# Every second wide block product of the FFNs multiplies the weights' low part first

## The chip, the cores and the metric

The kernel runs on one core of a Trainium2 chip. The metric is the device time of one execution in microseconds, the median of the runs of one measurement. Before the change it is 969.28 us (three runs, 968.81 to 969.39). The profile is of one further execution.

## The reference: what is computed

The input is a sequence of 512 tokens of 1024 channels in float32. Two decoder layers run over it. Each has a mixer (a gated convolution and pooling in the first, a gated MLP in the second) and then a gated FFN with 2816 hidden channels, and both add to the running state `h`. The change touches the FFNs alone:

```python
def gated_conv_ffn(x, w_gate, w_up, conv_w, conv_b, w_down):
    g = jnp.einsum('bsd,df->bsf', x, w_gate)
    g = causal_dwconv3(g, conv_w) + conv_b
    up = jnp.einsum('bsd,df->bsf', x, w_up)
    return jnp.einsum('bsf,fd->bsd', jax.nn.silu(g) * up, w_down)
```

So there are two products of 512 tokens by 1024 channels by 2816 hidden channels (gate, called `g` in the kernel, and up, called `u`), a convolution over three tokens, a silu, an elementwise product and a product back to 1024 channels (down).

## The kernel before: tiles, stages and order

**Two parts per number.** Matmuls take operands of the type float32r. Each operand is held as a high part (`hi`) and a rest (`lo`), and a product is the sum of three: hi by hi, hi by lo and lo by hi. The fourth, lo by lo, is left out.

**Block products.** The gate and up products are made with seven multiplications of half-size blocks instead of eight (a Strassen scheme). One block of work is a pair of hidden tiles, named by its first tile `f` = 2, 4, ..., 20 (`Ffn.products`, L885). In it each of `g` and `u` has seven products, so there are 14, in the order written in the loop at L920 to L922: g1, u1, g2, g5, g6, u5, u6, g7, u2, u7, g3, u3, g4, u4. The contraction of one product runs over four tiles of 128 channels (`NP` = 4, index `kp`). Weights stand in TensorE (they are what LDWEIGHTS loads, 128 by 128); activations stream through, and the result has 128 hidden channels by 256 tokens.

**Wide and narrow matmuls.** A product in the narrow form (L675 to L681) has twelve matmuls of 256 columns, all into one half of a PSUM bank. The wide form (L667 to L674, when `both` is given) uses that the hi and lo part of an activation lie side by side: four matmuls of 512 columns multiply the weights' hi part by both at once, and put hi by hi in the left half of the bank and hi by lo in the right half (L669). Then four matmuls of 256 columns multiply the weights' lo part by the activations' hi part into the left half (L672). Below, a wide matmul is one of 512 columns and a narrow one is one of 256. The halves are added afterwards by VectorE or by a copy on ScalarE and an add on VectorE (L905 and L917).

**Which products are wide.** `in_both` (L898) decides by `f`. In the first FFN all 14 products are wide for `f` = 8 to 20, in the second for `f` = 6 to 20, which makes 15 blocks. In one more block of each FFN (`f` = 6 and `f` = 4) the seven of `g` and u2, u5 and u3 are wide and the other four of `u` are narrow.

**Banks.** A product goes to bank `a`, `b` or `e` of its key (`BANK`, L652): 1, 6, 7 and 4 share `a`, 5 and 3 share `e`, and 2 has `b`. Later products add onto what is there; the first into a bank starts it anew.

**Where the low parts come from.** `Ffn.prepare` (L832) splits the weights of the next block while the current one is multiplied. ScalarE makes the hi parts. The lo parts are made by VectorE (`halves`, L828: the tiles `wlo_a`, `wlo_s12u`, `wlo_s34u`) or by a negated copy on ScalarE and an adding DMA from the POOL queue (L144 to L146 and L860 to L862: `wlo_g`, `wlo_u`, and for `g` also `wlo_s12g` and `wlo_s34g`).

**Order.** A tile scheduler sorts the instructions of each engine from its own estimate of when operands are ready; only what is put in `inorder` keeps the written order. So matmuls of neighbouring products can change places. After each block of work come matmuls of the down product (`half_down`, `mm3` at L159 to L161), all of 512 columns: 48 in a row after most blocks.

Of the kernel before, what the change touches and what calls it, by code (L numbers as in the profile page):

```python
# [31 lines left out]
def tile_trunk(ctx: ExitStack, tc: tile.TileContext, x, norm_mix, norm_ffn, final_norm,  # L32
# [3 lines left out]
    nc = tc.nc  # L36
# [9 lines left out]
    def mm_bank(name):  # L46
        return ps_mm.tile([P, 512], F32, tag="mm", name=name)
# [242 lines left out]
    def padded_tile():  # L290
        turn[0] += 1
        return padded[turn[0] % NPADDED]
# [296 lines left out]
    def project_blocks(name, w, acts, sums, norm, spare):  # L589
# [37 lines left out]
        for product in (1, 2, 5, 6, 3, 7, 4):  # L627
            for i in range(2):
                hi, lo = stat[product]
                c = slice(i * P, (i + 1) * P)  # L630
                if product == 3:
                    banks[i].pop("e")
                ps = multiply(banks[i], f"{name}_{product}{i}", product,
                              lambda kp: (hi[:, kp, c], lo[:, kp, c]),
                              lambda kp: moving(product, kp))
                for row, half in onto[product]:
                    d = h[4 + i + row][:, half * HALF : (half + 1) * HALF]
                    nc.vector.tensor_tensor(d, ps, d, ALU.add)
                if product in (3, 4):
                    norm.add(4 + i + 2 * (product == 4))  # L640
# [5 lines left out]
    NP = NK // 2  # L646
# [6 lines left out]

    last_matmul = [None]

    def multiply(banks, name, product, left, right, both=None):

        at = BANK[product]
        first = at not in banks
        if first:
            banks[at] = mm_bank(f"{name}{at}")
        ps = banks[at][:, :HALF]
        if both is not None:  # L667
            for kp in range(NP):
                nc.tensor.matmul(banks[at], left(kp)[0], both(kp), start=first and kp == 0,  # L669
                                 stop=kp == NP - 1, skip_group_check=True)  # L670
            for kp in range(NP):
                last_matmul[0] = nc.tensor.matmul(ps, left(kp)[1], right(kp)[0], start=False,  # L672
                                                  stop=kp == NP - 1, skip_group_check=True)
            return banks[at]  # L674
        for kp in range(NP):  # L675
            (a_hi, a_lo), (b_hi, b_lo) = left(kp), right(kp)
            for l, r, end in ((a_hi, b_hi, False), (a_hi, b_lo, False),
                              (a_lo, b_hi, kp == NP - 1)):
                nc.tensor.matmul(ps, l, r, start=first, stop=end, skip_group_check=True)  # L679
                first = False  # L680
        return ps  # L681
# [8 lines left out]
    class Ffn:  # L690
# [124 lines left out]
                return self.t41both[kp][:, :, product - 4, :]  # L815
            return hg2[kp + NP * (product > 1)][:, :, HALF * (product == 3) :][:, :, :HALF]

        def multiply(self, banks, name, product, weights_, both):
            hi, lo = weights_
            return multiply(banks, name, product, lambda kp: (hi[:, kp, :], lo[:, kp, :]),  # L820
                            lambda kp: self.moving(product, kp),
                            (lambda kp: self.moving_both(product, kp)) if both else None)

        def unit(self, name):
            return [wp.tile([P, 2, 4, P], F32R, tag=f"w{x}", bufs=6, name=f"w{x}_{name}")
# [59 lines left out]
        def products(self, f, stat):  # L885

            layer, ap, n = self.layer, self.ap, f"{self.layer}_{f}"
            banks = {"g": {}, "u": {}}
            kept = ap.tile([P, 3, HALF], F32, tag="kept", bufs=1, name=f"kept{n}")
            pads = [padded_tile() for _ in range(2)]  # L890
            lo, hi = slice(2, 2 + HALF), slice(2 + HALF, 2 + S)
            dst = {("g", 1): pads[0][:, lo], ("g", 6): pads[0][:, hi], ("g", 7): pads[1][:, hi],
                   ("g", 4): pads[1][:, lo]}
            dst.update({("u", product): kept[:, i, :] for i, product in enumerate((1, 6, 7))})
            onto = {2: 1, 7: 7, 3: 6}
            s = {}

            def in_both(key, product):  # L898
                first = FIRST_WIDE[layer]
                return f >= first[key] or f == first["g"] and product in (2, 5, 3)  # L900

            def add(d, bank, halves):
                ins = None
                for half in halves:
                    ins = nc.vector.tensor_tensor(d, bank[:, half * HALF : (half + 1) * HALF], d,  # L905
                                                  ALU.add)
                return ins

            def after(key, product, bank):
                halves = range(1 + in_both(key, product))  # L910
                if product in onto:
                    ins = add(dst[key, onto[product]], bank, halves)
                    if product == 7:
                        self.added[key] = ins
                elif (key, product) != ("u", 4):
                    d = dst[key, 7 if product == 5 else product]
                    nc.scalar.copy(d, bank[:, :HALF])  # L917
                    add(d, bank, halves[1:])

            for key, product in (("g", 1), ("u", 1), ("g", 2), ("g", 5), ("g", 6), ("u", 5),  # L920
                                 ("u", 6), ("g", 7), ("u", 2), ("u", 7), ("g", 3), ("u", 3),
                                 ("g", 4), ("u", 4)):  # L922
                bank = self.multiply(banks[key], f"{key}{n}", product, stat[key, product],
                                     in_both(key, product))
                after(key, product, bank)
                if (key, product) in (("g", 4), ("g", 3)):
                    j = product == 4
                    row = pads[j][:, 2:]
                    nc.vector.tensor_tensor(row, row, self.r, ALU.mult)  # L929
                    s[j] = self.silu(self.conv(pads[j], f + j), f + j)  # L930
                    if j and layer == 0:
                        nc.vector.tensor_tensor(s[1], s[1], self.r, ALU.mult)
            if layer == 0:
                nc.vector.tensor_tensor(kept[:, :2, :], kept[:, :2, :],
                                        self.r.rearrange("p (a b) -> p a b", a=2), ALU.mult)
            s0 = s[0].rearrange("p (a b) -> p a b", a=2)
            nc.vector.tensor_tensor(s0, kept[:, :2, :], s0, ALU.mult)
            nc.vector.tensor_tensor(s[1][:, HALF:], kept[:, 2, :], s[1][:, HALF:], ALU.mult)
            last = bank[:, :HALF]
            if in_both("u", 4):  # L940
                last = kept[:, 0, :]
                nc.scalar.copy(last, bank[:, :HALF])
                add(last, bank, (1,))
            nc.vector.tensor_tensor(s[1][:, :HALF], last, s[1][:, :HALF], ALU.mult)
            return [(f + 1, s[1]), (f, s[0])]
# [632 lines left out]
```

## Time and profile before

| what | value |
|---|---|
| median of three runs | 969.28 us |
| the profiled execution | 968.74 us |
| its span, first to last instruction | 967.0 us |
| TensorE matmul (PE) busy | 957.9 us, 5152 matmuls |
| weight loads (PEld) busy | 826.4 us |
| VectorE (DVE) / ScalarE (ACT) / GpSimd (POOL) busy | 847.5 / 622.7 / 161.6 us |
| granted TensorE clock, mean | 0.998 |

The profiled execution has 1.74 us around its span. A matmul's busy time overlaps that of the next one (a matmul of 512 columns is shown as 390 ns, though the next starts 227 ns after it in the longest stretches), so what a matmul takes from the stream is read from one start to the next start, in the timeline. A timeline row gives start, duration, engine, line, operation, output and inputs, shape and how many equal instructions it merges.

### The profile page before, as it was taken

The numbers are of one execution on the slowest core, as the hardware profiler recorded it, in microseconds if no ns is written. First come the engines' busy times: TensorE is split into PE (matmuls) and PEld (weight loads), VectorE is DVE, ScalarE is ACT, GpSimd is POOL, SyncE is SP. The second block draws the span as 40 slices with busy tenths as digits, with TensorE's granted clock in tenths as the row PEclk, the third lists the DMA queues.
The fourth block names the chain that finished last, engine by engine and source line by source line (L and its number), as shares of the span: only waits on it lengthen the run. The fifth ranks groups of instructions, "written<-read, shape, count | busy, mean of one in ns | idle before, by whom it ended". The sixth has DMA issues, their size and how long they took to land.

```text
span 967.0 us, 14196 instructions
## 1 busy us (share of the span) xinstructions
PE 957.9 (99%) x5152; PEld 826.4 (85%) x5152; DVE 847.5 (88%) x1435; ACT 622.7 (64%) x940; POOL 161.6 (17%) x183
## 2 busy tenths in 40 slices
PE   9999999999999999999999999999999999999996
PEld 7888898998888888888888888989888888888885
DVE  6887988989899898998878689899998989889898
ACT  5524667766576565765586847787665666656775
POOL 2141333111011010110311002311111011100123
PEclk9999999999999999999999999999999999999999
DMA  7442355787677677774352323567767777668775
GB/s 253 149 137 87 66 147 119 180 191 187 160 177 179 149 176 191 170 176 136 130 152 87 109 88 87 144 143 175 188 148 190 190 175 174 160 162 202 182 166 141
DMA packets 95825, 150.45 MB, mean 156 GB/s; under 512 B 5284, under 2 KB 61580, under 8 KB 95756
## 3 DMA queue, kind: packets, MB, share of 16 engines
q1 hardware_dynamic: 78284, 98.69, 32.5%
q0 software_dynamic: 15696, 49.03, 28.3%
q10 hardware_dynamic: 1776, 1.84, 0.6%
q8 instruction: 40, 0.66, 0.3%
q14 instruction: 29, 0.24, 0.1%
HBM read 98.42 MB, written 2.10 MB: 104 GB/s over the span
## 4 chain that ended last, share of the span: by engine, by line
PE 99%; DVE 1%; issue 0%; ACT 0%; POOLq 0%; DVEq 0%; POOL 0%
PE dn L160 3%; PE d L160 3%; PE dn L161 3%; PE d L159 3%; PE dn L159 3%; PE d L161 3%; PE vu_a L1127 2%; PE gu L159 2%; PE gu L161 2%; PE gu L160 2%; PE u_2a L679 1%; PE u_4a L679 1%; PE g_2a L679 1%; PE vu_e L1127 1%; PE dn_a L1426 1%; PE g_6a L669 1%
## 5 line engine op out<-in xcount | busy, mean ns | idle before, releaser
L146 POOL DMA_DIRECT2D wlo_g<-raw_g x20 | 17.2, 859 | 324.4 <-DVE kept L905 188.6
L715 DVE SCALAR_TENSOR_TENSOR c<-rows,prm,c 128x512 f32<-128x512 f32 x88 | 65.8, 749 | 1.1 <-ACT c L713 1.0
L160 PE MATMUL dn<-wlo_dn,a_hi 128*128 128x512 f32 x144 | 56.2, 391 | 0.0
L160 PE MATMUL d<-a_lo,whi_d 128*128 128x512 f32 x144 | 56.2, 390 | 0.0
L161 PE MATMUL dn<-whi_dn,a_lo 128*128 128x512 f32 x144 | 56.2, 390 | 0.0
L161 PE MATMUL d<-a_hi,wlo_d 128*128 128x512 f32 x144 | 56.2, 390 | 0.0
L159 PE MATMUL d<-a_hi,whi_d 128*128 128x512 f32 x144 | 56.2, 390 | 0.0
L159 PE MATMUL dn<-whi_dn,a_hi 128*128 128x512 f32 x144 | 56.1, 390 | 0.0
L829 ACT ACTIVATE whi_a<-raw_g 128x512 fp32r<-128x512 f32 x20 | 12.6, 632 | 61.3 <-PE g_8e L669 8.5
L144 ACT ACTIVATE wlo_g<-raw_g 128x1024 fp32r<-128x1024 f32 x20 | 21.2, 1062 | 26.4 <-PE g_2e L679 7.6
L1332 DVE SCALAR_TENSOR_TENSOR y<-dn,small,y 128x512 f32<-128x512 f32 x40 | 28.0, 749 | 8.6 <-PE dn L161 8.6
L713 ACT ACTIVATE c<-rows,prm 128x512 f32<-128x512 f32 x44 | 31.4, 715 | 5.3 <-DVE rows L929 5.3
L723 ACT ACTIVATE s<-c,prm 128x512 f32<-128x512 f32 x44 | 31.4, 716 | 3.4 <-DVE c L715 3.4
L268 ACT ACTIVATE a_hi<-s 128x512 fp32r<-128x512 f32 x40 | 24.8, 627 | 12.1 <-PE d L161 10.0
L204 ACT ACTIVATE hg<-h,prm 128x512 fp32r<-128x512 f32 x24 | 17.2, 718 | 23.5 <-DVE h L317 16.9
L155 DVE TENSOR_TENSOR wlo_dn<-raw_dn,whi_dn 128x1024 fp32r<-128x1024 f32 x18 | 22.0, 1224 | 11.7 <-ACT whi_dn L154 11.7
L161 PEld LDWEIGHTS dn<-whi_dn,a_lo 128*128 128x128 f32 x144 | 27.0, 188 | 5.7
L161 PEld LDWEIGHTS d<-a_hi,wlo_d 128*128 128x128 f32 x144 | 27.0, 188 | 5.7
L159 PEld LDWEIGHTS dn<-whi_dn,a_hi 128*128 128x128 f32 x144 | 27.1, 188 | 5.4
L159 PEld LDWEIGHTS d<-a_hi,whi_d 128*128 128x128 f32 x144 | 27.1, 188 | 5.3
L160 PEld LDWEIGHTS dn<-wlo_dn,a_hi 128*128 128x128 f32 x144 | 27.0, 188 | 5.4
L160 PEld LDWEIGHTS d<-a_lo,whi_d 128*128 128x128 f32 x144 | 27.1, 188 | 5.3
(1271 smaller groups left out, 3380.9 us busy)
## 6 DMA issues: line engine op xcount, KB each, us to landing
raw_g<-in_w_ffn_gate_dram SPq DMA_DIRECT2D x40, 512.0 KB, 3.8
raw_u<-in_w_ffn_up_dram SPq DMA_DIRECT2D x40, 512.0 KB, 4.7
raw_dn<-in_w_ffn_down_dram SPq DMA_DIRECT2D x22, 512.0 KB, 6.0
wlo_g<-raw_g POOLq DMA_DIRECT2D x20, 512.0 KB, 4.5
wlo_u<-raw_u POOLq DMA_DIRECT2D x20, 512.0 KB, 6.0
raw_d<-in_w_ffn_down_dram SPq DMA_DIRECT2D x18, 512.0 KB, 4.2
wlo_s12g<-s12g POOLq DMA_DIRECT2D x18, 512.0 KB, 6.3
wlo_s34g<-s34g POOLq DMA_DIRECT2D x18, 512.0 KB, 5.4
```

The lines of the kernel that those rows point to most:

```text
L144: first = nc.scalar.activation(lo, raw, AF.Copy, scale=-1.0)
L155: behind(nc.vector.tensor_tensor(lo, raw, hi.bitcast(F32), ALU.subtract), after[0])
L159: nc.tensor.matmul(ps, lhs[0], rhs[0], start=start, stop=False)
L160: nc.tensor.matmul(ps, lhs[0], rhs[1], start=False, stop=False)
L161: nc.tensor.matmul(ps, lhs[1], rhs[0], start=False, stop=stop)
L268: nc.scalar.activation(hi, src, AF.Copy, scale=scale)
L679: nc.tensor.matmul(ps, l, r, start=first, stop=end, skip_group_check=True)
L713: nc.scalar.activation(c, t[:, 0:S], AF.Copy, scale=prm("cf", ft))
L715: self.last_conv = nc.vector.scalar_tensor_tensor(c, t[:, i : S + i], prm("cf", i * NF + ft), c, op0=ALU.mult, op1=ALU.add)
L723: self.last_silu = nc.scalar.activation(s, c, AF.Silu, bias=self.prm("bf", ft))
L1127: nc.tensor.matmul(banks[at], lhs[l], rhs[r], start=first, stop=end, skip_group_check=True)
L1332: return nc.vector.scalar_tensor_tensor(dst, ps, ffn.cols[:, t : t + 1], dst, op0=ALU.mult, op1=ALU.add)
```

## The change

In every product with an odd index in the list of 14 (u1, g5, u5, g7, u7, u3, u4) the wide form is turned round: the four narrow matmuls of the lo part go first, then the four wide ones of the hi part. Products with an even index keep wide first. The first matmul of the product, whichever it is, starts a new bank. Products in the narrow form ignore the new argument. The number of matmuls, their operands, sizes and banks stay.

```diff
-    def multiply(banks, name, product, left, right, both=None):
+    def multiply(banks, name, product, left, right, both=None, low_first=False):
...
         if both is not None:
-            for kp in range(NP):
-                nc.tensor.matmul(banks[at], left(kp)[0], both(kp), start=first and kp == 0,
-                                 stop=kp == NP - 1, skip_group_check=True)
-            for kp in range(NP):
-                last_matmul[0] = nc.tensor.matmul(ps, left(kp)[1], right(kp)[0], start=False,
-                                                  stop=kp == NP - 1, skip_group_check=True)
+            for low in (low_first, not low_first):
+                for kp in range(NP):
+                    last_matmul[0] = nc.tensor.matmul(
+                        ps if low else banks[at], left(kp)[low],
+                        right(kp)[0] if low else both(kp), start=first, stop=kp == NP - 1,
+                        skip_group_check=True)
+                    first = False
             return banks[at]
...
-            for key, product in (("g", 1), ("u", 1), ("g", 2), ("g", 5), ("g", 6), ("u", 5),
-                                 ("u", 6), ("g", 7), ("u", 2), ("u", 7), ("g", 3), ("u", 3),
-                                 ("g", 4), ("u", 4)):
+            for i, (key, product) in enumerate((
+                    ("g", 1), ("u", 1), ("g", 2), ("g", 5), ("g", 6), ("u", 5), ("u", 6),
+                    ("g", 7), ("u", 2), ("u", 7), ("g", 3), ("u", 3), ("g", 4), ("u", 4))):
                 bank = self.multiply(banks[key], f"{key}{n}", product, stat[key, product],
-                                     in_both(key, product))
+                                     in_both(key, product), i % 2 == 1)
```

`Ffn.multiply` (L818) only hands the argument on. In the program as built, the lists of POOL and of SP (the DMA queue) are the same as before. Of VectorE's and ScalarE's, a few instructions change places, all in the blocks `f` = 4 to 8 of the second FFN. TensorE's list changes in the 17 blocks with wide products: in a block of 14 wide ones the runs of four wide and four narrow matmuls become runs of eight narrow and eight wide, with four wide ones at the start and at the end, which join the matmuls of the down product on either side. In three blocks of the first FFN (`f` = 10, 14, 18) the scheduler puts one wide matmul of u2 ahead of g7, so that one run of eight narrow is cut in two; in `f` = 6 of the second it puts u5 and g6 into each other.

More of the change, by code (lines that the diff above doesn't have):

```diff
@@ L816, in moving_both, with multiply @@
             return hg2[kp + NP * (product > 1)][:, :, HALF * (product == 3) :][:, :, :HALF]
-        def multiply(self, banks, name, product, weights_, both):
+        def multiply(self, banks, name, product, weights_, both, low_first):
             hi, lo = weights_
@@ L821, in multiply @@
                             lambda kp: self.moving(product, kp),
-                            (lambda kp: self.moving_both(product, kp)) if both else None)
+                            (lambda kp: self.moving_both(product, kp)) if both else None,
+                            low_first)
         def unit(self, name):
```

## The prediction

> **What bounds the kernel now.** I read the page first: span, busy times, granted clock, chain.
>
> ```profile
> span 967.0 us, 14196 instructions
> PE 957.9 (99%) x5152; PEld 826.4 (85%) x5152; DVE 847.5 (88%) x1435; ACT 622.7 (64%) x940; POOL 161.6 (17%) x183
> PEclk9999999999999999999999999999999999999999
> PE 99%; DVE 1%; issue 0%; ACT 0%; POOLq 0%; DVEq 0%; POOL 0%
> ```
>
> TensorE is the chain from end to end, at full clock. Busy 99% could still hide waits, so next come the waits of PE and of its weight loads.
>
> ```profile
> PE clock L61 <- DVE idle L56: 1.3, 1, 1.3
> PEld g_6a L669 <- DVE rows L905: 0.3, 1, 0.3
> ```
>
> One wait at the very start and one in the FFN blocks; nothing else keeps TensorE waiting in those blocks. So time can only come from how fast matmul follows matmul, and only a change of that by the order of wide (512 columns) and narrow (256 columns) can pay. I therefore read the timeline of PE, start to start, in a block where all 14 products are wide (`f` = 8, first FFN), and in the down products (L159 to L161) behind it.
>
> ```profile
> 247.91 1.07 PE L669 MATMUL g_8a<-hg,whi_a 128*128 128x512 f32 x4
> 248.81 0.64 PE L672 MATMUL g_8a<-hg,wlo_a 128*128 128x256 f32 x4
> 249.28 1.09 PE L669 MATMUL u_8a<-hg,whi_a 128*128 128x512 f32 x4
> 250.22 0.63 PE L672 MATMUL u_8a<-hg,wlo_a 128*128 128x256 f32 x4
> 250.69 1.09 PE L669 MATMUL g_8b<-hg,whi_g 128*128 128x512 f32 x4
> 251.61 0.64 PE L672 MATMUL g_8b<-hg,wlo_g 128*128 128x256 f32 x4
> ...
> 264.72 1.09 PE L669 MATMUL g_8a<-t,whi_g 128*128 128x512 f32 x4
> ...
> 267.53 0.40 PE L159 MATMUL d<-a_hi,whi_d 128*128 128x512 f32 x1
> ...
> 269.38 0.39 PE L161 MATMUL d<-a_hi,wlo_d 128*128 128x512 f32 x1
> 269.61 0.39 PE L159 MATMUL d<-a_hi,whi_d 128*128 128x512 f32 x1
> ```
>
> Ten products lie between 250.69 and 264.72: 14.03/10 = 1.403 us each, 2.806 us for two. The first four wide ones (247.91 to 248.81), which follow wide ones, take 0.90 us; all later fours, which follow narrow ones, take 0.92 to 0.94. A wide matmul is dearer behind narrow ones. For how long?
>
> ```profile
> 237.00 0.40 PE L159 MATMUL d<-a_hi,whi_d 128*128 128x512 f32 x1
> ...
> 237.93 0.39 PE L160 MATMUL d<-a_lo,whi_d 128*128 128x512 f32 x1
> 238.16 0.39 PE L161 MATMUL d<-a_hi,wlo_d 128*128 128x512 f32 x1
> ```
>
> Those are wide ones behind a run of 16 narrow. The first five take 1.16 us. From 238.16 to 247.91 (row above) the other 43 of the 48 take 9.75 us, 226.7 ns each. That is the settled step; the five cost 1.16 - 5 x 0.2267 = 0.026 us more. I call this the **short toll**, paid once and over after five. Behind the block of four-and-four there is a **long toll**: from 267.53 to 269.61 nine wide take 2.08 us against 2.04 settled, 0.04 us more. So the toll depends on what ran before.
>
> And the narrow ones, in longer runs, and eight wide in a row, which the scheduler happened to make in block `f` = 6:
>
> ```profile
> 218.02 0.64 PE L672 MATMUL g_6a<-hg,wlo_a 128*128 128x256 f32 x4
> 218.49 0.40 PE L679 MATMUL u_6a<-hg,whi_a 128*128 128x256 f32 x2
> ...
> 219.93 1.09 PE L669 MATMUL g_6b<-hg,whi_g 128*128 128x512 f32 x4
> ...
> 222.74 1.09 PE L669 MATMUL u_6e<-t,whi_s12u 128*128 128x512 f32 x4
> 223.67 1.07 PE L669 MATMUL g_6a<-t,whi_s12g 128*128 128x512 f32 x4
> 224.58 0.64 PE L672 MATMUL g_6a<-t,wlo_s12g 128*128 128x256 f32 x4
> ...
> 226.97 0.63 PE L669 MATMUL u_6b<-hg,whi_u 128*128 128x512 f32 x2
> ```
>
> Four narrow behind settled wide ones take 0.47 us (218.02 to 218.49), the next twelve 1.44 us, 0.12 each. Eight wide behind narrow take 1.84 us (222.74 to 224.58): 8 x 0.2267 = 1.814 plus the short toll of 0.026. Their second four take 0.91, settled again. The 20 narrow behind them take 2.39 us, 0.12 each.
>
> **The change part by part.** It adds and removes no matmul, weight load, copy, DMA or queue entry. It moves 113 times four narrow matmuls ahead of four wide ones: 7 in each of 15 blocks and 4 in each of two mixed blocks. In a full block the stream becomes 4 wide, then 8 narrow, 8 wide and so on, ending on 4 wide that run on into the down products.
>
> *The pair of products.* Before 2.806 us. After: 8 narrow, 0.47 + 4 x 0.12 = 0.95 (0.952 by nanoseconds), and 8 wide, 1.84: 2.79 us. So 14 ns less. What goes is one of two tolls per pair; what comes is that all narrow steps after the first of eight cost the full 0.12.
>
> *The full block, with its edges.* Before: 267.53 - 247.91 = 19.62, plus the long toll of 0.04 that the down products pay: 19.66. After: 4 settled wide 0.907, seven runs of 8 narrow 6.664, six runs of 8 wide 11.04, the last 4 wide 0.907, and one short toll of 0.026 there and in the down products: 19.54. Gain 0.12 us. Times 15 blocks: 1.8 us.
>
> *The mixed blocks and exceptions.* The two mixed blocks have four turned products each, partly between long narrow runs; by the same steps 0.02 to 0.1 us together. Three blocks of the first FFN get one wide matmul put between two fours of narrow, which costs some 0.02 us each. These cancel. Sum: **-1.8 us**.
>
> *Bounds of the new runs.* No run of exactly 8 narrow between wide runs is in the trace. The nearest rows are the 16 and the 20 above, 0.12 per step; a floor is half a settled wide step, 0.113. At the floor a pair saves another 45 ns, 4.7 us over 105 pairs; nothing in the trace comes near it over eight, and I take 0.119, the mean of the 16 (1.91/16). For 8 wide the ends are 1.84 (short toll, seen) and 1.85 (long toll: 267.53 to 269.38).
>
> *What the moved matmuls wait for.* The lo weights of an odd product are now asked for 0.93 us (four wide) sooner. Behind a waiting matmul stands the whole PE queue, so a late one would cost in full. The tightest cover that I find is u5 of block 6 in the second FFN; a typical DMA-made part stands below it.
>
> ```profile
> 698.63 1.22 DVE L830 TENSOR_TENSOR wlo_s12u<-s12u,whi_s12u 128x1024 fp32r<-128x1024 f32 x1
> 701.49 1.09 PE L669 MATMUL u_6e<-t,whi_s12u 128*128 128x512 f32 x4
> 243.50 0.86 POOL L861 DMA_DIRECT2D wlo_s34g<-s34g  x1 [4.64 <-ACT wlo_s34g L860]
> DMA to landing us min/median/max: 4.9/4.9/4.9
> 257.70 1.09 PE L669 MATMUL g_8a<-t,whi_s34g 128*128 128x512 f32 x4
> ```
>
> VectorE is done at 699.85 and the product starts at 701.49: 1.6 us of cover are left. The DMA issued at 243.50 lands by 248.4; g7 starts at 257.70. So this costs nothing while VectorE stays that far ahead. Banks are read at the same points as before, because each product still ends after its eighth matmul; the lo weights come free a little sooner and the hi weights no later. Nothing else is late next: POOL's and SP's lists do not change.
>
> **Sum.** The profiled execution is 968.74 us (span 967.0), which becomes 966.9. The median of the runs shown, 969.28, lies 0.54 above the profiled one; the same -1.8 makes it **967.5 us**, -0.19%.
>
> **The rivals.**
>
> *The order is worth nothing.* If a step belonged to a matmul's own width, pairs would stay at 2.806 us and the median at 969.3. This is also that the change doesn't do what it says. The Trainium skill, page "TensorE: Matmul & The Clock Gate", section "Back-to-back issue gap", gives such a rule: at full clock, columns by 2.4 plus 2.5 ns, whatever stands next to it (215.8 and 109.2 ns, an estimate of 1.30 us per product in either order). The trace does not agree: settled steps are 226.7 ns, and they grow behind narrow ones (0.90 against 0.94 us for four). Chance 0.05.
>
> *The long toll stays.* If eight narrow leave the stream as the blocks of now leave it, the eight wide take 1.85 to 1.86 and a pair 2.81: +3 ns or less a pair, and the block ends with the long toll as now. Time 969.3 to 969.6. For it: the long toll follows runs of four narrow that themselves follow unsettled wide ones. Against it: behind eight wide the stream is settled (0.91), and each run of 16 in the rows above left only the short toll. Chance 0.09.
>
> *More than forecast.* Narrow steps nearer 0.117 over eight would save another 16 ns a pair, 1.7 us: 965.8. Chance 0.10.
>
> *Slower: the lo part comes late.* Place: the products whose low part VectorE makes, u1, u5, u7 and u3, 60 in the full blocks. Price: the one late wait that the trace has in a block, where VectorE's L905 held up g7 of `f` = 6.
>
> ```profile
> 227.49 1.20 PE L669 MATMUL g_6a<-t,whi_s34g 128*128 128x512 f32 x4
> 228.52 0.63 PE L672 MATMUL g_6a<-t,wlo_s34g 128*128 128x256 f32 x4
> ```
>
> From 226.97 to 228.52 six wide take 1.55 instead of 1.36 + 0.03, so 0.16 us. It decides from the point at which VectorE (88% busy) falls back by the 1.6 us of cover; 11 such waits eat the gain, and all 60 make 9.6 - 1.8 = +7.8, 977.1 us. Against: VectorE's list is the same in all but three blocks. Chance 0.06.
>
> **How the numbers follow.** Forecast case 0.70 (gain 1.3 to 2.3 us, 967.0 to 968.0), more than that 0.10, no order effect 0.05, long toll 0.09, slower 0.06. About 0.2% (1.94 us) is what a measurement of this kernel can tell from no change, so 967.34 parts faster from same. It lies inside the forecast case: I give 0.27 of its 0.70 to the faster side. Faster 0.27 + 0.10 = 0.37, same 0.43 + 0.05 + 0.09 = 0.57, slower 0.06. The range from 966.3 to 968.9 holds the forecast case with the scatter of the runs (0.3 us either way) and the near half of the larger gain; it leaves out the no-gain cases and the slower one.
>
> **What would show it.** In the timeline of the changed kernel: runs of eight narrow of 0.95 us; runs of eight wide of 1.84, the second four 0.91; block 8 from its first matmul to the first down product some 0.08 us shorter and the down products' first nine 0.04 shorter. PE's waits in the blocks stay at the one of now. Wrong if fours of wide keep 0.93 in their second half, if narrow steps pass 0.12, or if new waits of PE or PEld on `wlo` tiles appear.

## The result and the profile after

| | before | after |
|---|---|---|
| median of 22 runs each | 969.49 us (968.56 to 970.36) | 967.91 us (966.99 to 968.87) |
| the profiled execution | 968.74 us | 968.03 us |
| its span | 967.0 us | 966.3 us |
| start of block `f` = 2, first FFN | 165.87 us | 166.71 us |
| from there to the last matmul's start | 793.34 us | 791.82 us |

The ratio of the times is 0.9985, with a 95% interval from 0.9979 to 0.9991: 1.58 us less, with 1.8 forecast (from the 969.28 of the first three runs of before). The spans differ by 0.7 us only, because the profiled execution of the changed kernel was 0.84 us later at the first FFN, before any changed instruction. That start lay between 165.69 and 166.77 us in the profiles of this study, so from here on traces are compared from the start of that block on: there the change takes 1.53 us off (unrounded).

The page of the changed kernel, the lines that stood first for before:

```profile
span 966.3 us, 14230 instructions
PE 957.6 (99%) x5152; PEld 827.2 (86%) x5152; DVE 847.0 (88%) x1435; ACT 620.7 (64%) x940; POOL 161.6 (17%) x183
PEclk9999999999999999999999999999999999999999
PE 99%; DVE 1%; issue 0%; POOLq 0%; DVEq 0%; POOL 0%; ACT 0%
```

The page hardly tells the two kernels apart: 34 instructions more, but the same number of matmuls, the same clock and the same chain. The difference shows only in the timeline of PE, read from start to start, in block `f` = 8 of the first FFN:

```profile
248.63 1.07 PE L670 MATMUL g_8a<-hg,whi_a 128*128 128x512 f32 x4
249.54 0.64 PE L670 MATMUL g_8a<-hg,wlo_a 128*128 128x256 f32 x4
250.01 0.64 PE L670 MATMUL u_8a<-hg,wlo_a 128*128 128x256 f32 x4
250.49 1.09 PE L670 MATMUL u_8a<-hg,whi_a 128*128 128x512 f32 x4
251.42 1.07 PE L670 MATMUL g_8b<-hg,whi_g 128*128 128x512 f32 x4
252.33 0.64 PE L670 MATMUL g_8b<-hg,wlo_g 128*128 128x256 f32 x4
...
268.18 0.39 PE L159 MATMUL d<-a_hi,whi_d 128*128 128x512 f32 x1
...
270.23 0.39 PE L159 MATMUL d<-a_hi,whi_d 128*128 128x512 f32 x1
```

Eight narrow take 0.95 us (249.54 to 250.49), eight wide 1.84 (250.49 to 252.33), and of these the first four 0.93 and the second four 0.91. The single steps of eight narrow are 113 or 114, 119 and six times 120 ns, those of eight wide 233, 236, 228, 233, 231, 226, 227, 227. The block lasts 268.18 - 248.63 = 19.55 us, where it was 19.62, and the first nine down products 2.05 instead of 2.08.

Two waits of weight loads in the changed kernel bear on the forecast:

```profile
PEld g_6a L670 <- DVE rows L907: 0.2, 1, 0.2
PEld vu_a L1129 <- ACT u L1146: 0.2, 1, 0.2
```

The first is the wait that before had too (0.3 there), at g7 of the mixed block `f` = 6. It has become shorter: the prediction read 0.16 us over for the six wide matmuls around it in before, and now it is the four narrow ones of g7 that take 0.53 instead of 0.47.

```profile
228.27 0.69 PE L670 MATMUL g_6a<-t,wlo_s34g 128*128 128x256 f32 x4
228.80 1.09 PE L670 MATMUL g_6a<-t,whi_s34g 128*128 128x512 f32 x4
```

The second is new. It stands in the mixer between the two FFNs, which the change doesn't touch; it makes the two matmuls from 530.61 last until 531.13, 0.52 us where two settled steps are 0.45.

In block `f` = 10 (as in 14 and 18) one wide u2 matmul stands ahead of g7 and cuts the run of eight narrow:

```profile
288.35 0.64 PE L670 MATMUL u_10a<-t,wlo_s12u 128*128 128x256 f32 x4
288.83 0.39 PE L670 MATMUL u_10b<-hg,whi_u 128*128 128x512 f32 x1
289.06 0.65 PE L670 MATMUL g_10a<-t,wlo_s34g 128*128 128x256 f32 x4
289.55 1.09 PE L670 MATMUL g_10a<-t,whi_s34g 128*128 128x512 f32 x4
```

The second four narrow take 0.49 us (289.06 to 289.55), the first of them 136 ns. Before had a wide u2 matmul ahead of g7 in this place, too:

```profile
288.25 0.39 PE L669 MATMUL u_10b<-hg,whi_u 128*128 128x512 f32 x1
288.48 1.08 PE L669 MATMUL g_10a<-t,whi_s34g 128*128 128x512 f32 x4
```

So these three blocks, and `f` = 6 of the second FFN, where two stood ahead of g7, were cheaper before than block 8: 19.59 to 19.61 us instead of 19.62, with 0.02 less in the stretch behind.

From the starts of the matmuls in both traces, in us, for each block and for the stretch behind it (down products and the first part of the next block):

| | block | stretch behind | together |
|---|---|---|---|
| ten full blocks (`f` = 8, 12, 16 of the first FFN, 8 to 20 of the second), each | -0.071 | -0.042 | -0.113 |
| `f` = 10, 14, 18 of the first | -0.022, -0.035, -0.037 | -0.025, -0.025, -0.023 | -0.167 |
| `f` = 20 of the first, with the mixer behind it | -0.071 | +0.038 | -0.033 |
| `f` = 6 of the second | +0.004 | -0.024 | -0.020 |
| the two mixed blocks | -0.114, -0.060 | 0 | -0.174 |
| sum | | | -1.53 |

### The profile page after: what moved, and what is told of

Its sections match the earlier page's. It is cut to its first block, busy times and chain, and to the rows that moved or that the text cites. A ratio compares the mean times of both kernels' runs of the same rounds, so it can differ in the third digit from the quotient of the medians.

```text
span 966.3 us, 14230 instructions
## 1 busy us (share of the span) xinstructions
PE 957.6 (99%) x5152; PEld 827.2 (86%) x5152; DVE 847.0 (88%) x1435; ACT 620.7 (64%) x940; POOL 161.6 (17%) x183
## 3 DMA queue, kind: packets, MB, share of 16 engines
q10 hardware_dynamic: 1776, 1.84, 0.6%
## 4 chain that ended last, share of the span: by engine, by line
PE 99%; DVE 1%; issue 0%; POOLq 0%; DVEq 0%; POOL 0%; ACT 0%
PE d L159 3%; PE d L160 3%; PE dn L159 3%; PE dn L160 3%; PE dn L161 3%; PE d L161 3%; PE vu_a L1129 2%; PE gu L159 2%; PE gu L161 2%; PE gu L160 2%; PE u_2a L680 1%; PE g_2a L680 1%; PE u_4a L680 1%; PE u_20a L670 1%; PE u_18a L670 1%; PE u_12a L670 1%
```

## The experiments

**Theory.** A matmul's step depends on its neighbours. A wide one behind narrow ones pays a toll over five steps, a narrow one behind a narrow one pays 6 to 7 ns over its columns' share; the change halves the number of meetings. **The rivals:** the gain comes from the order in which the low parts or the banks are asked for (waits), not from the lengths of the runs; or a meeting costs a whole toll each time, however short the runs.

In the table the second column is the trace's difference to before from the first FFN's block `f` = 2 to the end, the third the difference of the medians.

| kernel | trace, us | medians, us | ratio, 95% interval |
|---|---|---|---|
| the change | -1.53 | -1.58 | 0.9985 (0.9979 to 0.9991) |
| one wide, one narrow in turn | +3.00 | +3.02 | 1.0030 (1.0018 to 1.0042) |
| two and two | -1.49 | -1.51 | 0.9983 (0.9974 to 0.9993) |
| low part first in every product | +1.71 | +1.78 | 1.0019 (1.0010 to 1.0028) |
| low part first in the even products | +1.05 | +0.28 | 1.0003 (0.9993 to 1.0012) |
| runs of sixteen | +0.17 | +0.39 | 1.0006 (0.9997 to 1.0016) |
| the change in its written order | +0.61 | +0.43 | 1.0005 (0.9995 to 1.0014) |
| the change, but sixteen in the second FFN | -1.75 | -1.74 | 0.9984 (0.9975 to 0.9993) |
| the change in the second FFN alone | -0.79 | -1.07 | 0.9991 (0.9982 to 1.0000) |

In eight of nine rows the two differences agree within 0.3 us, so the blocks and stretches of a trace account for the times. In the row that differs by 0.77 us the profiled execution was the longest of its ten (970.49, median 969.72), so the waits read from it below are likely larger than those of the median run. Where the interval holds 1.0000, the medians don't part the kernel from before.

### One and one

```diff
-            for low in (low_first, not low_first):
-                for kp in range(NP):
+            for kp in range(NP):
+                for low in (False, True):
```

> In every wide product one wide matmul and one narrow matmul alternate, over the four tiles of the contraction. Theory (a narrow step costs 0.12 us only from the second or third narrow matmul in a row on, and the toll on wide ones is owed to a run of several narrow ones): each lone narrow step is near the 0.113 to 0.114 us of the first in a run, each wide step 0.227 to 0.233, so a product takes 1.36 to 1.39 us against 1.403 before, and the kernel is 3 to 10 us faster than before the change. Rival (each passage from narrow to wide costs a toll of 0.026 us, however short the run): four tolls per product instead of one, 1.46 us per product, about 13 us slower than before. Rival (the order is worth nothing): 1.403, no change.

972.46 us against 969.44, 3.0 us slower. The timeline of PE in block `f` = 12 of the first FFN:

```profile
310.28 0.39 PE L670 MATMUL g_12a<-hg,whi_a 128*128 128x512 f32 x1
310.50 0.28 PE L670 MATMUL g_12a<-hg,wlo_a 128*128 128x256 f32 x1
310.62 0.40 PE L670 MATMUL g_12a<-hg,whi_a 128*128 128x512 f32 x1
...
320.17 0.50 PE L670 MATMUL g_12a<-t,whi_s34g 128*128 128x512 f32 x1
320.50 0.28 PE L670 MATMUL g_12a<-t,wlo_s34g 128*128 128x256 f32 x1
...
324.50 0.39 PE L670 MATMUL g_12e<-hg,whi_s34g 128*128 128x512 f32 x1
...
330.04 0.39 PE L159 MATMUL d<-a_hi,whi_d 128*128 128x512 f32 x1
```

Up to g7 the narrow steps are 113 to 120 ns, but no wide one settles: 232 to 241 each. Three pairs take 1060 ns, so a product 1.413 us. Then the first wide matmul of g7 takes 0.33 us (320.17 to 320.50), because its weight load waits until VectorE has read the bank (L907). From u7 on the same order runs in another pattern, wide steps of 230 and narrow ones of 116 or 117 ns: the last four products take 5.54 us (324.50 to 330.04), 1.385 each. The block takes 19.76 instead of 19.62.

So the theory's price, 1.36 to 1.39 us per product, stands in one part of the block and not in the other; what starts the second pattern is not shown. It comes up in ten of the 15 full blocks. The wait at g7 (in four of them one at u7 too) stands in 12 of the 15, 1.3 us together. The forecast of a faster kernel fell, then, partly by waits and not by the price of the meetings alone. The full toll at each meeting, 1.46 us per product, was seen in neither pattern.

### Two and two

```diff
-            for low in (low_first, not low_first):
-                for kp in range(NP):
-                    last_matmul[0] = nc.tensor.matmul(
...
+            for low, kp in ((0, 0), (0, 1), (1, 0), (1, 1), (0, 2), (0, 3), (1, 2), (1, 3)):
+                last_matmul[0] = nc.tensor.matmul(
```

> In every wide product two wide, two narrow, two wide, two narrow. Theory: two narrow in a row take 0.113 + 0.119 or 0.116 + 0.112, two wide behind them 0.463 to 0.469; a product is 1.39 us against 1.403 before, and the kernel some 2.5 us faster than before, about 1 us faster than the change. Rival (a full toll of 0.026 us at each passage): 1.42 us per product, about 4 us slower than before.

967.93 us, 1.5 less than before: as much as the change, with wide first in every product and four times as many meetings. The timeline of PE, block `f` = 8 of the first FFN:

```profile
248.50 0.40 PE L669 MATMUL g_8a<-hg,wlo_a 128*128 128x256 f32 x2
248.74 0.63 PE L669 MATMUL g_8a<-hg,whi_a 128*128 128x512 f32 x2
249.20 0.39 PE L669 MATMUL g_8a<-hg,wlo_a 128*128 128x256 f32 x2
249.43 0.63 PE L669 MATMUL u_8a<-hg,whi_a 128*128 128x512 f32 x2
249.90 0.40 PE L669 MATMUL u_8a<-hg,wlo_a 128*128 128x256 f32 x2
```

Two narrow take 0.23 us and two wide 0.46 to 0.47; the single steps go 113 and 119, 233 and 236, 116 and 113, 232 and 231. Per product that is 33 ns over settled steps, against 43 for four and four (41 and 46 in turn). It gave 1 us less than expected; 0.45 of that is the first wide matmul of a g7 or u7, which takes 272 to 279 ns in eleven blocks, and 0.18 a wait in the mixer. So the count of meetings alone doesn't set the price: a run of two ends before the whole toll is paid and before the narrow steps have grown.

### Which products are turned

```diff
-                                     in_both(key, product), i % 2 == 1)
+                                     in_both(key, product), True)
```

> Every wide product multiplies the low part first, so runs of four narrow and four wide matmuls alternate as before the change, only the other way round inside each product. Theory (run lengths alone count): two products take 2.806 us again, block 8 of the first FFN 19.6 us, and the time is that of before within 0.3 us. Rival (multiplying the low part first is worth something by itself, 14 ns for each of the 113 turned products): all 230 turned, 3.2 us faster than before.

```diff
-                                     in_both(key, product), i % 2 == 1)
+                                     in_both(key, product), i % 2 == 0)
```

> The products with an even index are turned instead of those with an odd one: a block starts and ends with four narrow, with runs of eight between them. Theory: runs of eight narrow 0.95 us, of eight wide 1.84 us, block 8 of the first FFN 19.55 us, about 1.5 us faster than before, the change's time within 0.3 us. Rival (it matters which products are turned, for instance because the turned ones of the change start a new bank with narrow matmuls): a gain clearly other than the change's.

All turned: 971.22 us, 1.8 slower; runs are of four again and block 8 is 19.64. Even ones turned: 969.72, no gain, though its runs are the change's (0.95 and 1.84 us, block 8 19.55). So the theory's count of meetings holds within the blocks, and something else takes the gain. The waits of weight loads in the kernel with the even products turned:

```profile
PEld vu_a L1129 <- ACT u L1146: 1.0, 1, 1.0
PEld g_14a L670 <- DVE rows L907: 1.0, 1, 1.0
PEld d_last L159 <- ACT a_hi L268: 0.7, 1, 0.7
```

With all turned the first two are there too, 1.0 and 0.6 us. The wait in block 14 in the timeline of PE and of VectorE, first of the kernel with the even products turned, then of the change:

```profile
349.67 0.28 PE L670 MATMUL u_14b<-hg,wlo_u 128*128 128x256 f32 x1
350.61 1.19 PE L670 MATMUL g_14a<-t,whi_s34g 128*128 128x512 f32 x4 [0.65 <-DVE rows L907]
...
348.99 1.23 DVE L832 TENSOR_TENSOR wlo_s34u<-s12u,whi_s34u 128x1024 fp32r<-128x1024 f32 x1 [0.46 <-ACT whi_s34u L831]
350.13 0.42 DVE L907 TENSOR_TENSOR rows<-g_14a,rows 128x256 f32<-128x256 f32 x1
```

```profile
347.10 1.22 DVE L832 TENSOR_TENSOR wlo_s34u<-s12u,whi_s34u 128x1024 fp32r<-128x1024 f32 x1 [0.16 <-ACT whi_s34u L831]
348.25 1.22 DVE L155 TENSOR_TENSOR wlo_d<-raw_d,whi_d 128x1024 fp32r<-128x1024 f32 x1
349.38 0.42 DVE L907 TENSOR_TENSOR rows<-g_14a,rows 128x256 f32<-128x256 f32 x1
```

No low part is late. g7 adds onto the bank that g6 filled, and must wait until VectorE has read g6's result from it (L907). VectorE does this in a fixed order. Where the even products are turned, the scheduler placed the making of the next parts otherwise, and the read starts at 350.13 instead of 349.38, though both traces enter the block within 0.06 us of each other. In the mixer it looks like the same kind of thing: ScalarE's first scaling of `h` (L1055) starts 2.34 us later than in the change (488.52 against 486.18), while PE's last block of the first FFN starts 0.97 us later (432.25 against 431.28). Between the two, VectorE still splits a part of `wlo_d_last` at 465.41, which the change has done by 460.51, and its fourth update of `h` from `d_last` (L317) starts 2.70 us later (475.66 against 472.96). How much each displaced instruction adds is not separated.

### How long is the toll? A stream with nothing else

The changed kernel with 489 matmuls added after the last product, in written order, with 16 wide before and behind each run; the last 48 have bf16 operands, all zeros. Their results are read by nobody. One profiled execution, 1054.98 us; from the first FFN to the end of the last block its blocks are those of the changed kernel within 0.03 us in all.

```diff
+    runs = [(256, n) for n in (1, 2, 3, 4, 5, 6, 8, 12, 16)]
+    runs += [(c, 12) for c in (128, 192, 240, 264, 272, 288, 320, 384)]
...
+    for c, n in runs:
+        steps += [c] * n + [512] * 16
```

> The changed kernel, with a stream of matmuls behind its last product whose results nobody reads: runs of 1, 2, 3, 4, 5, 6, 8, 12 and 16 matmuls of 256 columns, then runs of 12 matmuls of 128, 192, 240, 264, 272, 288, 320 and 384 columns, each behind 16 of 512 columns, all of one tile of the 32-bit format; then 16 of 512, 16 of 256 and 16 of 512 columns in bf16. Theory (a step has a floor of 0.12 us, set by the load of 128 columns of weights in the 32-bit format; matmuls that stream for less than that bring the toll on): steps of 0.12 us for every width up to 264, of 0.4427 ns a column from 272 on (0.128, 0.142, 0.170 us for 288, 320, 384), the short toll of 0.026 us behind every run of 4 or more matmuls up to 264 columns, less behind 1 to 3, and none behind 288 to 384. In bf16 neither the 0.12 nor the toll. Rival (the toll is owed to a change of width as such): a toll behind 288, 320 and 384 columns and in bf16 as well. Rival (a narrow matmul has its own price, not a floor): 128 and 192 columns take clearly less than 0.12.

The added groups by line, with the shortest, median and longest duration:

```profile
L1561 PEld LDWEIGHTS probe<-hg x441: 187/188/192, 958.4 to 1043.0; 128*128 128x128 f32 x147
L1566 PEld LDWEIGHTS <-flat x48: 96/98/100, 1043.5 to 1051.7; 128*128 128x128 bf16 x48
```

Durations hide the steps (a matmul of 512 columns is shown as 389 ns at the median), so these are from the starts of the single matmuls, in ns; "over" is the excess above 226.7 ns for 512 columns, or the share of it.

| run of 256 columns | 1 | 2 | 3 | 4 | 5 | 6 | 8 | 12 | 16 |
|---|---|---|---|---|---|---|---|---|---|
| sum of the run | 114 | 233 | 352 | 473 | 593 | 712 | 953 | 1433 | 1912 |
| over | 1 | 6 | 12 | 20 | 26 | 32 | 46 | 73 | 99 |
| over, 16 wide behind it | 26 | 27 | 27 | 27 | 27 | 27 | 27 | 27 | 27 |

| run of 12, columns | 128 | 192 | 240 | 256 | 264 | 272 | 288 | 320 | 384 |
|---|---|---|---|---|---|---|---|---|---|
| mean step | 107 | 110 | 112 | 119 | 120 | 126 | 132 | 146 | 176 |
| share by columns | 57 | 85 | 106 | 113 | 117 | 120 | 128 | 142 | 170 |
| over, wide ones behind it | 111 | 35 | 42 | 27 | -2 | 38 | 48 | 25 | 40 |

Behind 256 columns the toll is 27 ns and is the same behind one narrow matmul as behind 16, with the steps 233, 236, 228, 233, 231. A run of n narrow costs some 6.6 ns over for each but the first. Together, per product of four and four: runs of eight (46 + 27)/2 = 36.5 ns, runs of sixteen (99 + 27)/4 = 31.5, four and four 43 in the kernel (20 + 27 = 47 here, where the toll is paid to its end), two and two 33 in the kernel. With 256 columns there is one toll, 27 ns. The "long toll" of the prediction, 40 ns, was seen with them only where the wide ones ahead had themselves been cut off before the fifth.

Of what was put forward, the floor of 0.12 us fell: 128 to 240 columns take 107 to 112 ns a step. So did the forecast that the toll ends above 264 columns: at 264 there is none, and 272 to 384 leave 25 to 48 ns. The rival, a toll at any change of width, holds in the 32-bit format but for 264 columns; in bf16 there is none.

### Runs of sixteen

Two neighbouring products give all their wide, then all their narrow matmuls, and the next two the other way round. For this u6 goes ahead of u5, and u2 ahead of g7.

```diff
+            order = (("g", 1), ("u", 1), ("g", 2), ("g", 5), ("g", 6), ("u", 6), ("u", 5),
+                     ("u", 2), ("g", 7), ("u", 7), ("g", 3), ("u", 3), ("g", 4), ("u", 4))
...
+            def pair(i):
+                flip = i // 2 % 2
+                for low in (flip, not flip):
+                    for key, product in order[i : i + 2]:
```

> Two neighbouring products are made together: the wide matmuls of both, then the narrow ones of both, and the next two the other way round, so that runs of 16 arise; u6, u5, u2, g7, u7 stand in another order so that no bank is read just before it is written again. Theory (run lengths alone count): 16 narrow take 1.91 us, 16 wide 3.65 us, block 8 of the first FFN 19.46 us against 19.55 in the change and 19.62 before, some 2.6 us faster than before and 0.9 faster than the change. Rival (waits take it back: products end in twos, and the readers of banks and the low weights of two products come together): runs as above but new waits of PE in the blocks, and no faster than the change.

969.85 us, 0.4 above before and no gain. The timeline of PE in block 8 has the runs, and the waits of weight loads have what took the gain:

```profile
254.17 1.07 PE L670 MATMUL g_8a<-t,whi_s12g 128*128 128x512 f32 x4
...
255.99 0.64 PE L670 MATMUL g_8a<-t,wlo_s12g 128*128 128x256 f32 x4
...
257.42 0.64 PE L670 MATMUL u_8b<-hg,wlo_u 128*128 128x256 f32 x4
257.90 1.09 PE L670 MATMUL u_8e<-t,whi_s12u 128*128 128x512 f32 x4
```

```profile
PEld u_14b L670 <- DMA wlo_u<-raw_u: 0.8, 1, 0.8
PEld vu_a L1148 <- ACT u L1165: 0.6, 1, 0.6
...
PEld u_18b L670 <- DMA wlo_u<-raw_u: 0.4, 1, 0.4
...
PEld u_10b L670 <- DMA wlo_u<-raw_u: 0.4, 1, 0.4
```

Sixteen narrow take 1.91 us (255.99 to 257.90), as in the stream alone, and the ten undisturbed full blocks gain 0.154 each and 0.019 behind them: 0.173, or 2.6 us over 15, what was expected. But u2 is now asked for sooner than its low part, which a DMA makes, has landed. Here the low part does come late, in the three blocks shown and, by 0.2, in `f` = 6 of the second FFN, and with the mixer's wait nothing is left.

### The written order

```diff
-                    last_matmul[0] = nc.tensor.matmul(
+                    last_matmul[0] = inorder(nc.tensor.matmul(
```

> The change with the wide products' matmuls kept in the written order, so that the scheduler puts no matmul of u2 ahead of g7 in blocks 10, 14 and 18 of the first FFN and does not mix u5 and g6 in block 6 of the second. Theory: these four blocks take 19.55 us like the others instead of 19.56 to 19.60, with the stretches behind them 0.02 shorter, 0.1 to 0.2 us in all, which the time hardly shows. Rival (the scheduler's swap covered a late reader of g's bank): g7 waits for VectorE's L907 in those blocks, 0.1 us or more each, and the kernel is no faster than the change or slower.

969.89 us, 0.4 above before and no gain. The waits of matmuls, and the timeline of PE in block `f` = 6 of the second FFN:

```profile
PE g_6a L670 <- DVE rows L907: 0.9, 2, 0.7
```

```profile
701.54 1.09 PE L670 MATMUL g_6e<-t,whi_s12g 128*128 128x512 f32 x4
703.30 1.15 PE L670 MATMUL g_6a<-t,whi_s12g 128*128 128x512 f32 x4 [0.66 <-DVE rows L907]
```

The clean blocks are those of the change (19.55). The blocks in which the scheduler had put a u2 or u5 matmul between now wait for the bank instead, against before: +0.34, +0.30, +0.18, +0.20 in `f` = 6, 10, 14, 18 of the first FFN, +0.86 in `f` = 6 of the second. So the mixing that cuts runs, counted as a small loss in the prediction, saves 2.1 us in the changed kernel (+0.61 against -1.53).

### Putting it together

The change in the first FFN and runs of sixteen in the second (the loop of the kernel above where `layer == 1`, the change's loop elsewhere):

> The changed kernel in the first FFN; in the second FFN runs of sixteen, with the product order of the run that had them in both. Theory (the toll is paid at each meeting of widths, and the rest is waits that come with the order of the whole list): the first FFN's blocks and stretches give what they gave in the changed kernel, -0.65 us, the second's what runs of sixteen gave there, blocks -0.97 and stretches -0.13, together -1.75 us against the kernel before, about 967.7 us. A clean block of the second FFN 19.47 us, of the first 19.55. Rival (the list is planned as a whole, so a change in one FFN moves waits in any place): the clean blocks as above, but new waits of 0.3 to 1.4 us each at the products g7 or in the mixer, and the total between 968 and 970.

And the change in the second FFN alone:

```diff
-                                     in_both(key, product), i % 2 == 1)
+                                     in_both(key, product), layer == 1 and i % 2 == 1)
```

> The change in the second FFN alone; the first FFN has the code of before. Theory: the first FFN's blocks stay at 19.59 to 19.62 us and its stretches at what they were, the second FFN gives what it gave in the changed kernel, blocks -0.55 and stretches -0.32, together -0.87 us, a ratio of 0.9991. Rival (the second FFN's gain hung on waits that the change in the first FFN had moved): a sum in the second FFN that differs from -0.87 by more than 0.2, or a difference in the first FFN's blocks although their code is unchanged.

The first is 967.84 us, 1.74 less than before; the trace gives -0.65 in the first FFN and -1.09 in the second, -1.75 in all, as expected to 0.02 us. It is the lowest median of the study, but 967.84 cannot be told from the change's 967.91. In its second FFN the runs are there (sixteen narrow from 728.31 to 730.22) and the low part of u2 is in time, except in `f` = 6 (+0.20):

```profile
728.31 0.64 PE L670 MATMUL g_8a<-hg,wlo_a 128*128 128x256 f32 x4
...
730.22 1.09 PE L670 MATMUL g_8b<-hg,whi_g 128*128 128x512 f32 x4
```

The second is 968.51 us. Its second FFN gives -0.87, to the hundredth what it gave in the change, and the blocks of the first are those of before within 0.014 us. In the mixer it has the new wait of 0.07 us, though ahead of it every engine's instructions stand in the order of before. So this small wait comes without any turned product ahead of it; whether it differs from one execution to the next was not tried. The gains of the runs add up block by block.

## Why the prediction was right, point by point

- **What bounds the kernel.** Right. TensorE's stream is the chain, and steps and waits of PE make up the time: in eight of nine kernels the sum of blocks and stretches is the difference of the medians within 0.3 us.
- **The pair of products.** Right. Eight narrow 0.952 or 0.953 us, eight wide 1.841, a pair 2.79. The bound left open, how eight narrow run, is 953 ns in the kernel and in the stream alone; the 0.119 chosen holds, and neither the floor of 0.113 nor 0.117 is reached.
- **The full block, with its edges.** The mechanism was right, the term a little large: 0.113 us and not 0.12, because 0.12 was the difference of two sums from rounded rows. Over 15 blocks that would be 1.70 instead of 1.80. But block 8 was taken for all 15: in four of them (`f` = 10, 14, 18 of the first FFN, 6 of the second) before was already 0.03 to 0.05 us cheaper each, 0.17 together, the same four in which u2 matmuls stood ahead of g7. The next point counts this.
- **The mixed blocks and exceptions.** The two mixed blocks gave 0.17, more than 0.02 to 0.1; 0.10 of it is the bank's wait at g7 of `f` = 6, which fell from 0.16 to 0.06 and which no step had, and the 0.07 left is in the range. The three cut blocks lost 0.17 against 0.113 each: 0.12 because before was cheaper there, and 0.05 by the cut itself, for which 0.06 was forecast (the first narrow step of g7, at the read of its bank, takes 127 to 136 ns instead of 113). The block `f` = 6 of the second FFN, with u5 and g6 in each other, gave 0.02 where 0.113 was counted; half of the 0.09 missing is its cheaper state before. It was named in the description of the change and not priced. The mixer's wait took back 0.08, in one execution of each kernel; the kernel with the change in the second FFN alone has it too. Together: 1.70 + 0.17 - 0.17 - 0.09 - 0.08 = 1.53. That terms left out of the sum stand on both sides and partly cancel is luck.
- **What the moved matmuls wait for.** For the change itself right: no wait on a low part in the trace. The cover was sought at the wrong neighbour, though. In four of the other orders (one and one, both kinds of turning, the written order) the first thing late in a block was the bank that VectorE had not yet read; the low part was late only where u2 was moved ahead of a product (0.2 to 0.8 us).
- **The rivals.** "The order is worth nothing" is refuted by the pair's 2.79 us and by the five rows of the table whose interval leaves out 1. "The long toll stays" is refuted by the second four of eight wide, 0.91 us. "More than forecast" needed narrow steps of 0.117 over eight. "The lo part comes late" did not happen here, but its like did in the kernels with other orders, at one to five times the price named for one wait (0.2 to 0.8 us against 0.16); there it was the part that a DMA makes.
- **The Trainium skill's rule** (page "TensorE: Matmul & The Clock Gate", section "Back-to-back issue gap", columns by 2.4 plus 2.5 ns, given there as the gap of a single matmul by itself) does hold for one part of the added stream: with bf16 operands, 512 columns step by 215.9 and 256 by 109.1 ns, with no toll when widths change, where it gives 215.8 and 109.2. In this kernel's float32r matmuls it does not.

## What to carry to other kernels

Where TensorE is the whole chain, price an order of wide and narrow matmuls from steps (start to start) and from the lengths of the runs, as a toll per meeting plus a growth per narrow step, and check that price in a stream with nothing else in it; with runs of one matmul the price was not fixed by the runs alone. Read the time before from each block's own rows, since a scheduler may have made some unlike the others. Then look for the waits that a new order brings outside the edited lines: with a scheduler that plans the whole list, a gain of 1.5 us in 969 is as easily taken back by one bank read, or one chain of a neighbouring stage, that falls a place back. Compare traces from a point behind the start-up, block by block, before believing or doubting a difference of spans.

## What the runs showed of the hardware that was not expected

- The toll of wide behind narrow doesn't depend on the number of narrow ones (27 ns behind one and behind 16), and it is gone behind 12 of 264 columns (-2 ns), while 12 of 240, 272 or 288 columns leave 38 to 48 ns. What the first five wide steps wait for stays open; no run here separates it.
- Below 256 columns a float32r step hardly falls: 112 ns at 240 columns and, after the first, 112 at 128. Its weight load lasts 188 ns against 98 for bf16, and bf16 steps follow the columns. That the weight load makes this floor fits, but was not tried by itself.
- At 256 columns the step is 120 ns, above both the 113 of its columns and the 112 at 240.
- One wide and one narrow in turn ran in two steady patterns in one block, 353 and 347 ns a pair. What holds the stream in the one or the other stays open.
